# Storing split weights right behind their last part, and adding the last product of gate and up into a bank already read

## The chip, the cores and the metric

The kernel runs on one core of one Trainium2 chip. The metric is device time in microseconds (us) of one execution; lower is better. A core has five engines that run their own instruction lists in order and wait for each other through semaphores: TensorE (PE), VectorE (DVE), ScalarE (ACT), GpSimd (POOL) and SyncE (SP). SP here issues nearly all DMA transfers, on one queue.

## The reference

One block of a transformer in float32: RMSNorm, a projection, differential attention and stick-breaking attention, an output projection, and a SwiGLU feed-forward part. The change touches the feed-forward part alone:

```python
u2 = rms_norm(h, norm2_w)                    # h: 2048 x 1024
gate = einsum('bsd,df->bsf', u2, w_gate)     # 1024 -> 2816
up = einsum('bsd,df->bsf', u2, w_up)         # 1024 -> 2816
h = h + einsum('bsf,fd->bsd', silu(gate) * up, w_down)
```

## The kernel before, in words

Float32 products are made of float16 ones: each operand is scaled by a power of two and split into a high and a low float16 part, and three of the four partial products are summed in PSUM. On top of that the feed-forward part uses a Strassen-like scheme of seven block products in place of eight. It is done in two halves of 1024 tokens. A half goes through eleven groups of 256 feed-forward columns (`fg`), and each group has three weights, called g, u and d after gate, up and down.

In the first half each weight is fetched from the inputs as float32 (`stage`, 1024 KB) into one of the two buffers of the tile `stages`, which the weights take in turn. ACT squares it (tile `sq`, L869 or L184), PE sums the squares of each column (tile `fsc`, L877, or L177 for d), DVE turns the sum into a power of two in some seven small operations (the last one that the split needs is L199), and then the seven block operands are made: high parts on ACT or POOL (L210 on ACT), low parts on DVE (L215), and sums and differences of blocks on POOL (L98, output `stages` or `sx`). The result (`wg`, `wu` or `wd`) is used at once, and is also stored to the DRAM tile `split` (1792 KB), from which the second half loads it without any splitting. A buffer of `stages` may be fetched into again when the last part that reads it is made.

Stores are held in a list, `keep`. A store leaves the list when two later weights have been begun, and it is then put on SP's queue directly behind the fetch just issued (`tc.issue_after`).

`quad` makes the seven products of gate or up for one group: `pa`, `pm`, `pm`, a second product into `pa`, then `pd`, `pm` and `pe`, of 12 matmuls each (L939; a product is 12 matmuls of 128x512). Each of them but the second into `pa` takes a fresh PSUM bank from `pst`, which hands out eight banks in turn. DVE adds the pieces: L952 and L956 for the `pm` pair, L966 reads `pd` into the block c22, L968 adds `pd` to u2, L971 takes the fourth product, L975 adds `pe` to u2. Each of the four finished blocks then goes to SiLU on ACT (gate, L986) or to a multiplication on DVE (up, L1006), and after up four more sums on DVE (L98, outputs `cu` and `cg`) make the operands of down (`act`, L1000 on ACT and L98 on POOL or DVE). Down runs for two or three groups at once (L1041), and its sums go through ACT (L1067), DVE (L1047) and POOL.

The order of the instructions on each engine isn't written by hand. A scheduler sets it from a model of times, and each engine then executes its list strictly in that order: an instruction that waits holds everything behind it.

Of the kernel before, what the change touches and what calls it, by code (L numbers as in the profile page):

```python
# [16 lines left out]
ALU = mybir.AluOpType  # L17
# [4 lines left out]
S, D, P = 2048, 1024, 128  # L22
NT, KT, NC = S // P, D // P, S // 512
FF = 2816
NFG = FF // 256
# [34 lines left out]
def block(tc, a, out):  # L60
    nc = tc.nc
    PE, ACT, DVE, POOL, SP = nc.tensor, nc.scalar, nc.vector, nc.gpsimd, nc.sync
    top = ExitStack()
    with top:
# [100 lines left out]
        split = dr.tile([NFG, 3, P, 7 * 2 * 512], F16, name="split")  # L165
# [637 lines left out]
        with ExitStack() as ph2:  # L803
# [18 lines left out]
            r_2, p_2, r_24 = rp2  # L822
            scales = {}

            keep, rows = [], []
            stages = fw.tile([P, 2, 2048], F32, name="stages", bufs=1)
            turn = [0]

            def stage(fg, nme):
                st = stages[:, turn[0]]  # L830
                turn[0] ^= 1
                f0 = 256 * fg
                with tc.issue_after(rows[1].ins) if (fg, nme) == (1, "u") else nullcontext():
                    d = fetch(st, f0, nme)
                if len(keep) > 1:
                    with tc.issue_after(d.ins):
                        SP.dma_start(*keep.pop(0))
                return st

            def fetch(st, f0, nme):  # L840
                if nme == "d":
                    return SP.dma_start(st.rearrange("p (f n) -> p f n", f=2), a["w_down"][0, f0 : f0 + 256, :].rearrange("(f p) n -> p f n", p=P))
                return SP.dma_start(st.rearrange("p (k n) -> p k n", k=KT), a["w_gate" if nme == "g" else "w_up"][0, :, f0 : f0 + 256].rearrange("(k p) n -> p k n", p=P))

            ones = fw.tile([P, P], BF16, name="ones", bufs=1)
            DVE.memset(ones[:], 1.0)
# [5 lines left out]
            def load_ffn(half, fg, names, W):  # L852
                eng = "ADP" if fg == 0 else WE
                sc = scales.setdefault(fg, {})
                for nme in names:
                    if half == 1:
                        yield
                        late = nme == "d" and fg == NFG - 1
                        w16 = (fd if nme == "d" and not late else fw).tile([P, 7, 2, 512], F16, tag="wd" if nme == "d" and not late else "wgu", bufs=2, name=nm("w" + nme))
# [3 lines left out]
                    st = stage(fg, nme)  # L863
                    r, p, sW = c1(), c1(), c1()
# [35 lines left out]
                    else:  # L900
                        sv = st.rearrange("p (d k f n) -> p d k f n", d=2, k=4, f=2)
                        xv = sx[:].rearrange("p (k n) -> p k n", k=4)
                        wv = w16[:].rearrange("p o s (k n) -> p o s k n", k=4)
# [11 lines left out]
                        putk(4, sv[:, :, :, 0, :], 2)  # L915
                        putk(6, xv.unsqueeze(1), 1)
                    W[nme] = w16
                    keep.append((split[fg, "gud".index(nme)], w16[:].rearrange("p o s n -> p (o s n)")))
                    if fg == NFG - 1 and nme == "d":
                        while keep:  # L920
                            SP.dma_start(*keep.pop(0))
                if half == 0 and "g" in names:
                    kg, F = c1(), c1()
                    times(kg, sc["g"][1], p_2, 2.0 ** -14)
# [10 lines left out]
            def product(ps_, wv, wo, X, xo, start, stop):  # L935
                q = 0
                for kt in range(4):
                    for xi, wi in ((0, 0), (1, 0), (0, 1)):
                        PE.matmul(ps_[:].rearrange("p (t n) -> p t n", n=P), lhsT=wv[:, wo, wi, 128 * kt : 128 * kt + 128], rhs=X[xo][:, :, xi, kt, :], start=start and q == 0, stop=stop and q == 11, skip_group_check=not start)  # L939
                        q += 1  # L940

            def quad(wv, X, tag, bufs, c11, hook=None):
                def cst():
                    return fp.tile([P, 512], F32, tag=tag, bufs=bufs, name=nm(tag))

                pa = pst("pa")
                product(pa, wv, 0, X, 0, True, True)
                u2 = cst()
                ACT.copy(u2[:], pa[:])
                p6 = pst("pm")  # L950
                product(p6, wv, 4, X, 4, True, True)
# [12 lines left out]
                product(pd, wv, 2, X, 2, True, True)  # L964
                c22 = cst()
                DVE.tensor_tensor(c22[:], pd[:], u3[:], ALU.add)  # L966
                c11(1, 1, c22)
                DVE.tensor_tensor(u2[:], u2[:], pd[:], ALU.add)  # L968
                p4 = pst("pm")
                product(p4, wv, 3, X, 6, True, True)  # L970
                DVE.tensor_tensor(u3[:], u3[:], p4[:], ALU.subtract)  # L971
                c11(1, 0, u3)
                p5 = pst("pe")
                product(p5, wv, 5, X, 3, True, True)
                DVE.tensor_tensor(u2[:], u2[:], p5[:], ALU.add)  # L975
                c11(0, 1, u2)

            def gate(W, X, hook=None):
# [256 lines left out]
```

## Time and profile before

| | us |
|---|---|
| median of 3 runs | 2778.39 (2778.34 to 2778.42) |
| the profiled execution | 2775.94 |
| its span, first to last instruction | 2774.2 |
| PE busy in the span | 2494.4 (90%) |
| DVE busy | 2008.2 (72%) |
| ACT busy | 1359.0 (49%) |
| POOL busy | 1428.7 (52%) |

Attention and the projections fill the span to about 1466 us, the first half of the feed-forward part goes to about 2190 us, the second to the end. The profile page says where time is lost on average; a table by stages (windows) says in which part, and the rows in order of time say which instruction waited for which. Times of rows are from the start of the span.

### The profile page before, as it was taken

The page shows a single profiled execution, that of the slowest core. Times are in us where ns is not written, and L with a number is a line of the kernel's source. Part 1 is how long each engine was busy: PE and PEld are TensorE (multiplying, and loading weights), DVE is VectorE, ACT ScalarE, POOL GpSimd, SP SyncE. Part 2 cuts the span into 40 slices and gives each one's busy share as a digit, 9 for nine tenths or more (in the row PEclk, how much of TensorE's full clock was granted, in tenths as well). Part 3 has the DMA queues.
Part 4 walks back from the last instruction along what each step waited for, and adds up shares of the span by engine and source line. Part 5 has one row for each costly group of instructions (what it writes and reads, how often), then busy time and mean ns, then how long its engine had stood idle before and what let it go on. Part 6 is the DMA issues. An engine that isn't in the chain of part 4 may idle for free.

```text
span 2774.2 us, 45434 instructions
## 1 busy us (share of the span) xinstructions
PE 2494.4 (90%) x17084; PEld 1409.7 (51%) x17084; DVE 2008.2 (72%) x3796; ACT 1359.0 (49%) x2539; POOL 1428.7 (52%) x1002
## 2 busy tenths in 40 slices
PE   6998989988888786888889898999899999999999
PEld 4655555555555454557775343444444444444444
DVE  6888879787989989875766877777776644444444
ACT  4665656466878878764644534343442211121120
POOL 2568767665544555546664656564645422322322
PEclk9999999999999997999999999999999999999999
DMA  7788787789999998997797565555648835535432
GB/s 228 198 165 183 145 190 162 173 172 203 198 209 195 199 181 160 191 195 208 198 309 258 199 222 200 197 203 197 231 172 284 349 141 193 205 126 205 183 121 92
DMA packets 646829, 543.52 MB, mean 196 GB/s; under 512 B 506368, under 2 KB 573952, under 8 KB 636368
## 3 DMA queue, kind: packets, MB, share of 16 engines
q1 hardware_dynamic: 644784, 538.53, 71.0%
q8 instruction: 134, 2.20, 0.3%
q0 software_dynamic: 512, 1.36, 0.2%
q10 hardware_dynamic: 1312, 0.72, 0.1%
q14 instruction: 87, 0.71, 0.1%
HBM read 261.08 MB, written 147.32 MB: 147 GB/s over the span
## 4 chain that ended last, share of the span: by engine, by line
PE 31%; DVE 9%; DMA 6%; issue 4%; ACT 3%; POOL 3%; SPq 0%; DVEq 0%; ACTq 0%; POOLq 0%
PE pd L1041 13%; PE pm L939 7%; PE pa L939 5%; PE pd L939 3%; DVE wd L215 2%; PE pe L939 2%; DMA stages<-in_w_gate_dram 2%; DMA stages<-in_w_down_dram 1%; DVE wu L215 1%; PE po L761 1%; DMA aT<-s 1%; DMA stages<-in_w_up_dram 1%; DVE cg L1006 1%; POOL s L98 1%; DVE wg L215 1%
## 5 line engine op out<-in xcount | busy, mean ns | idle before, releaser
L98 POOL TENSOR_TENSOR s<-z,s 128x1024 f16<-128x1024 f32 (+7 forms) x288 | 473.8, 1653 | 336.0 <-ACT s L89 300.0
L320 PE MATMUL pj<-w,xt 128*128 128x384 f16 x3072 | 573.9, 335 | 26.9 <-DVE st L330 11.6
L320 PEld LDWEIGHTS <-xt 128*128 128x128 f16 x3072 | 300.5, 100 | 237.6 <-issue 38.7
L1041 PE MATMUL pd<-wd,act 128*128 128x512 f16 x1764 | 395.4, 382 | 20.2 <-ACT cu L1067 16.9
L448 PE MATMUL sc<-kT,qT 128*128 128x512 f16 (+3 forms) x1280 | 347.9, 362 | 69.8 <-DVE z L558 30.9
L557 DVE TENSOR_TENSOR_SCAN z<-z,sc 128x512 f32<-128x512 f32 (+3 forms) x320 | 355.8, 1113 | 66.2 <-ACT sc L555 62.8
L458 PE MATMUL yp<-v,aT 128*128 128x64 f16 (+1 forms) x4896 | 282.5, 208 | 83.1 <-DMA aT<-s 82.2
L458 PEld LDWEIGHTS <-aT 128*128 128x128 f16 x4896 | 245.7, 102 | 174.3 <-DMA aT<-s 111.6
L939 PEld LDWEIGHTS <-wu 128*128 128x128 f16 x1848 | 182.2, 99 | 243.4 <-issue 12.8
L98 POOL TENSOR_TENSOR act<-cg,act 128x512 f16<-128x512 f32 x109 | 152.7, 1411 | 284.4 <-ACT act L1000 284.4
L939 PEld LDWEIGHTS <-wg 128*128 128x128 f16 x1848 | 181.1, 98 | 221.0 <-issue 6.4
L1041 PEld LDWEIGHTS <-act 128*128 128x128 f16 x1764 | 173.5, 98 | 232.0 <-issue 27.7
L89 ACT CAST s<-z 128x384 f16<-128x384 f32 (+7 forms) x216 | 170.4, 789 | 151.7 <-DMA aT<-s 64.2
L98 POOL TENSOR_TENSOR stages<-stages 128x512 f32<-128x512 f32 x97 | 171.6, 1770 | 129.0 <-DVE wd L215 47.0
L98 POOL TENSOR_TENSOR hs<-hs,cu 128x512 f32<-128x512 f32 x102 | 133.0, 1312 | 188.2 <-DVE cu L1047 64.6
L554 ACT ACTIVATE z<-sc,c 128x512 f32<-128x512 f32 (+3 forms) x320 | 203.1, 635 | 12.6 <-PE sc L448 10.8
L939 PE MATMUL pm<-X,wu 128*128 128x512 f16 x792 | 186.8, 390 | 18.2 <-ACT wu L210 10.8
L1000 ACT CAST act<-cg 128x512 f16<-128x512 f32 x126 | 77.7, 618 | 250.8 <-DVE cg L1006 202.7
L558 DVE TENSOR_TENSOR z<-sc,z 128x512 f32<-128x512 f32 (+3 forms) x320 | 193.6, 607 | 8.1
L555 ACT ACTIVATE sc<-sc,c 128x512 f32<-128x512 f32 (+3 forms) x320 | 195.3, 610 | 0.0
L1047 DVE SCALAR_TENSOR_TENSOR hs<-pd,c,hs 128x512 f32<-128x512 f32 x144 | 105.8, 748 | 118.4 <-PE pd L1041 110.3
L761 PE MATMUL po<-wo,mt 128*128 128x256 f16 x1536 | 180.9, 275 | 9.2 <-DVE xf L764 4.8
(245 smaller groups left out, 4140.7 us busy)
## 6 DMA issues: line engine op xcount, KB each, us to landing
xt<-xs SPq DMA_DIRECT2D x112, 512.0 KB, 4.3
hs<-hd SPq DMA_DIRECT2D x72, 512.0 KB, 4.4
hd<-hs SPq DMA_DIRECT2D x56, 512.0 KB, 5.2
split<-wg SPq DMA_DIRECT2D x11, 1792.0 KB, 10.6
split<-wu SPq DMA_DIRECT2D x11, 1792.0 KB, 10.4
split<-wd SPq DMA_DIRECT2D x11, 1792.0 KB, 10.9
wg<-split SPq DMA_DIRECT2D x11, 1792.0 KB, 7.2
wd<-split SPq DMA_DIRECT2D x11, 1792.0 KB, 9.2
```

Source lines behind the costliest of these rows:

```text
L89: ACT.copy(dst, src)
L98: (DVE if e == "D" else POOL).tensor_tensor(dst, a_, b_, op)
L320: PE.matmul(pj[:, :384], lhsT=xv[:, xi, kt, :], rhs=G["w"][:, wi, kt, :], start=n == 0, stop=n == 23)
L448: PE.matmul(sc[:, : 128 * w].rearrange("p (t n) -> p t n", n=P), lhsT=G["q"][i // 4][:, 2 - 2 * o + m, i % 4, :], rhs=G["k"][q][:, m, 0:w, ...
L458: PE.matmul(yp[:, y0 : y0 + wd], lhsT=aT[:, a_, :], rhs=v[:, v_ : v_ + wd], start=start and j == 0 and q == 0, stop=stop and j == nb - 1 a ...
L554: ACT.activation(om[:, lo:hi], sc[:, :w], AF.Sigmoid, scale=G["nkz"][:])
L555: ACT.activation(sc[:, :w], sc[:, :w], AF.Sigmoid, scale=G["kz"][:])
L557: DVE.tensor_tensor_scan(ov, ov, sc[:, :w], om[:, hi : hi + 1], op0=ALU.mult, op1=ALU.bypass)
L558: DVE.tensor_tensor(be[:, lo:hi], sc[:, :w], om[:, lo + 1 : hi + 1], ALU.mult)
L761: PE.matmul(po[:, sl], lhsT=mt[:, kt, P * xi : P * xi + P], rhs=wos[2 * h + n][wi][:, kt, :], start=q == 0, stop=q == 23)
L939: PE.matmul(ps_[:].rearrange("p (t n) -> p t n", n=P), lhsT=wv[:, wo, wi, 128 * kt : 128 * kt + 128], rhs=X[xo][:, :, xi, kt, :], start=st ...
L1041: PE.matmul(po[:], lhsT=act[:, ao, xi, 128 * j : 128 * j + 128], rhs=W["d"][:, wo, wi, :], start=start and u == 0 and q == 0, stop=u == nu ...
```

## The change

Two edits. A store of a split weight is issued where the split ends in the program, without the list and without a place on the queue behind a fetch. And the last product of `quad` is added by PE into `pd`, which DVE has read for c22 by then; the separate addition of `pd` to u2 (old L968) goes, the addition of `pe` to u2 becomes one of `pd` (new L968), and `quad` takes five banks instead of six.

```diff
-            keep, rows = [], []
+            rows = []
...
                 with tc.issue_after(rows[1].ins) if (fg, nme) == (1, "u") else nullcontext():
-                    d = fetch(st, f0, nme)
-                if len(keep) > 1:
-                    with tc.issue_after(d.ins):
-                        SP.dma_start(*keep.pop(0))
+                    fetch(st, f0, nme)
                 return st
...
                     W[nme] = w16
-                    keep.append((split[fg, "gud".index(nme)], w16[:].rearrange("p o s n -> p (o s n)")))
-                    if fg == NFG - 1 and nme == "d":
-                        while keep:
-                            SP.dma_start(*keep.pop(0))
+                    SP.dma_start(split[fg, "gud".index(nme)], w16[:].rearrange("p o s n -> p (o s n)"))
...
                 c11(1, 1, c22)
-                DVE.tensor_tensor(u2[:], u2[:], pd[:], ALU.add)
                 p4 = pst("pm")
                 product(p4, wv, 3, X, 6, True, True)
                 DVE.tensor_tensor(u3[:], u3[:], p4[:], ALU.subtract)
                 c11(1, 0, u3)
-                p5 = pst("pe")
-                product(p5, wv, 5, X, 3, True, True)
-                DVE.tensor_tensor(u2[:], u2[:], p5[:], ALU.add)
+                product(pd, wv, 5, X, 3, False, True)
+                DVE.tensor_tensor(u2[:], u2[:], pd[:], ALU.add)
                 c11(0, 1, u2)
```

The scheduler makes a new order of it on every engine of the feed-forward part. Lines of the changed kernel have other numbers: L837 (store) is L916, L841 and L839 are the fetches, L961 is the old L966, L965 the old L971, L999 the old L1006, L867 the old L869.

SP's queue in the first half, from the fetch of a gate weight on, before:

```order
L843 DMA stages<-in_w_gate_dram 128x8x256
L837 DMA split<-wd_23047 128x7168
L842 DMA stages<-in_w_down_dram 128x2x1024
L837 DMA split<-wu_23145 128x7168
L843 DMA stages<-in_w_up_dram 128x8x256
L837 DMA split<-wg_23287 128x7168
```

and now:

```order
L916 DMA split<-wd_23022 128x7168
L841 DMA stages<-in_w_gate_dram 128x8x256
L916 DMA split<-wu_23118 128x7168
L839 DMA stages<-in_w_down_dram 128x2x1024
L916 DMA split<-wg_23258 128x7168
L841 DMA stages<-in_w_up_dram 128x8x256
```

Fetch and store have changed places in each pair: the same store stood behind the fetch and now stands ahead of it.

DVE at the end of up, where the parts of `wd` are made between the sums of up, before:

```order
L966 TENSOR_TENSOR cu_22150<-pd_22137,cu_22086 128x512
L968 TENSOR_TENSOR cu_22057<-cu_22057,pd_22137 128x512
L215 SCALAR_TENSOR_TENSOR wd_22103<-stages,c_21913,wd_22103 128x2x512
L1006 SCALAR_TENSOR_TENSOR cg_21711<-cu_22150,c_21430,cg_21711 128x512
L215 SCALAR_TENSOR_TENSOR wd_22103<-stages,c_21913,wd_22103 128x2x512
L215 SCALAR_TENSOR_TENSOR wd_22103<-sx_22113,c_21913,wd_22103 128x512
L971 TENSOR_TENSOR cu_22086<-cu_22086,pm_22156 128x512
L975 TENSOR_TENSOR cu_22057<-cu_22057,pe_22173 128x512
L1006 SCALAR_TENSOR_TENSOR cg_21675<-cu_22086,c_21430,cg_21675 128x512
L878 TENSOR_REDUCE m_22203<-fsc_22202 128x1
L1006 SCALAR_TENSOR_TENSOR cg_21646<-cu_22057,c_21430,cg_21646 128x512
L215 SCALAR_TENSOR_TENSOR wd_22103<-stages,c_21913,wd_22103 128x2x512
```

and now:

```order
L961 TENSOR_TENSOR cu_22133<-pd_22120,cu_22069 128x512
L215 SCALAR_TENSOR_TENSOR wd_22086<-stages,c_21896,wd_22086 128x2x512
L999 SCALAR_TENSOR_TENSOR cg_21696<-cu_22133,c_21418,cg_21696 128x512
L215 SCALAR_TENSOR_TENSOR wd_22086<-stages,c_21896,wd_22086 128x2x512
L215 SCALAR_TENSOR_TENSOR wd_22086<-sx_22096,c_21896,wd_22086 128x512
L965 TENSOR_TENSOR cu_22069<-cu_22069,pm_22138 128x512
L876 TENSOR_REDUCE m_22184<-fsc_22183 128x1
L999 SCALAR_TENSOR_TENSOR cg_21661<-cu_22069,c_21418,cg_21661 128x512
L195 TENSOR_SCALAR m_22184<-m_22184 128x1
L215 SCALAR_TENSOR_TENSOR wd_22086<-stages,c_21896,wd_22086 128x2x512
L170 TENSOR_SCALAR c_22116<-m_22184 128x1
L968 TENSOR_TENSOR cu_22040<-cu_22040,pd_22120 128x512
```

The sum into u2 and the multiplication behind it (L968 and an L999) now stand behind the last part of `wd`, not ahead of it.

ACT a little later, while gate of the next group runs and the parts of `wu` are made, before:

```order
L949 COPY cg_22244<-pa_22231 128x512
L1000 CAST act_22043<-cu_22188 128x512
L1000 CAST act_22043<-cg_21646 128x512
L1000 CAST act_22043<-cg_21689 128x512
L869 ACTIVATE sq_22294<-stages 128x2048
L1000 CAST act_22043<-cg_21675 128x512
L210 ACTIVATE wu_22201<-stages,c_22134 128x2x512 x2
L210 ACTIVATE wu_22201<-sx_22218,c_22134 128x512
L986 ACTIVATE cg_22287<-pa_22231,c_21905 128x512
L986 ACTIVATE cg_22309<-cg_22309,c_21905 128x512
L210 ACTIVATE wu_22201<-stages,c_22134 128x2x512
```

and now:

```order
L993 CAST act_22026<-cu_22169 128x512
L210 ACTIVATE wu_22182<-stages,c_22117 128x2x512 x2
L210 ACTIVATE wu_22182<-sx_22199,c_22117 128x512
L993 CAST act_22026<-cg_21632 128x512
L993 CAST act_22026<-cg_21675 128x512
L993 CAST act_22026<-cg_21661 128x512
L979 ACTIVATE cg_22269<-pa_22213,c_21889 128x512
L867 ACTIVATE sq_22275<-stages 128x2048
L210 ACTIVATE wu_22182<-stages,c_22117 128x2x512
```

The squares of the gate weight (`sq`), which wait for its fetch, now stand behind the first parts of `wu`. The parts of `wd` that follow pass the squares of the next up weight in the same way: all of them in every second stretch, all but the last one in the others. On PE the last product of `quad` stands later in the list: 3 to 11 matmuls of the following product or of down come ahead of it.

More of the change, by code (lines that the diff above doesn't have):

```diff
@@ L841, in fetch @@
                 if nme == "d":
-                    return SP.dma_start(st.rearrange("p (f n) -> p f n", f=2), a["w_down"][0, f0 : f0 + 256, :].rearrange("(f p) n -> p f n", p=P))
-                return SP.dma_start(st.rearrange("p (k n) -> p k n", k=KT), a["w_gate" if nme == "g" else "w_up"][0, :, f0 : f0 + 256].rearrange("(k p) n -> p k n", p=P))
+                    SP.dma_start(st.rearrange("p (f n) -> p f n", f=2), a["w_down"][0, f0 : f0 + 256, :].rearrange("(f p) n -> p f n", p=P))
+                else:
+                    SP.dma_start(st.rearrange("p (k n) -> p k n", k=KT), a["w_gate" if nme == "g" else "w_up"][0, :, f0 : f0 + 256].rearrange("(k p) n -> p k n", p=P))
             ones = fw.tile([P, P], BF16, name="ones", bufs=1)
```

## The prediction

> **What bounds the kernel now.** I first read the table by stages, because the change touches the feed-forward part alone (columns: stretch, length, busy us and count of PE, PEld, DVE, ACT, POOL; granted clock, DMA share, GB/s).
>
> ```profile
> span 2774.2 us, 45434 instructions
> ...
> 1700.00:1800.00 100.00, 91.27 (x427) 42.04 (x427) 76.12 (x111) 40.50 (x49) 57.81 (x38) 0.98 0.59 206
> 1800.00:1900.00 100.00, 93.36 (x435) 43.13 (x433) 71.34 (x102) 39.14 (x46) 59.29 (x39) 0.97 0.63 223
> 1900.00:2000.00 100.00, 88.62 (x411) 40.31 (x409) 80.15 (x112) 44.93 (x55) 61.36 (x40) 0.97 0.55 187
> ...
> 2300.00:2400.00 100.00, 100.00 (x465) 45.37 (x464) 45.08 (x59) 18.97 (x30) 29.16 (x23) 1.00 0.49 177
> ```
>
> The second half is PE without a gap. The first half leaves PE idle for 7 to 11 us in 100, with no other engine full, so something there is late. The rows of PE in order of time name it (start, us, instruction, and in brackets the idle time ahead and what ended it). They are one stretch: up of one group, gate and up of the next, gate again, then down.
>
> ```profile
> 1794.07 0.60 PE L939 MATMUL pm<-X,wu 128*128 128x512 f16 x2 [2.88 <-ACT wu L210]
> ...
> 1796.46 6.36 PE L939 MATMUL pm<-X,wu 128*128 128x512 f16 x22 [1.78 <-DVE wu L215]
> ...
> 1816.06 1.03 PE L877 MATMUL fsc<-sq,ones 128*128 128x256 bf16 x8 [1.15 <-ACT sq L869]
> ...
> 1839.82 1.24 PE L1041 MATMUL pd<-wd,act 128*128 128x512 f16 x5 [0.93 <-ACT cg L986]
> ...
> 1845.61 13.18 PE L1041 MATMUL pd<-wd,act 128*128 128x512 f16 x49 [4.55 <-ACT cu L1067]
> ```
>
> That is 11.3 us of waiting in a stretch, all for weights being split or for ACT behind them. There are five such stretches. The chain of waits shows what the weights wait for (start, us, what):
>
> ```profile
> 1758.15 2.59 PE pa L939 x12
> ...
> 1777.28 6.60 DMA stages<-in_w_gate_dram
> ...
> 1796.43 6.44 DMA stages<-in_w_down_dram
> ...
> 1807.36 6.66 DMA stages<-in_w_up_dram
> ...
> 1830.48 6.71 DMA stages<-in_w_gate_dram
> ```
>
> Four fetches of a stretch lie on the chain. Each starts the moment its buffer's last part is made, so the weights go round: fetch, squares, scale, parts, fetch. A product of 12 matmuls takes PE 2.59, or 0.216 a matmul.
>
> **The second half: nothing.** The edit to the sums applies there too. The rows of one product and its readers:
>
> ```profile
> 2310.56 2.75 PE L939 MATMUL pm<-X,wu 128*128 128x512 f16 x12
> ...
> 2310.82 0.69 DVE L966 TENSOR_TENSOR cu<-pd,cu 128x512 f32<-128x512 f32 x1 [1.89 <-PE pd L939]
> ```
>
> DVE has read `pd` by 2311.5, and the product ahead of the last one runs to 2313.15. That covers the new wait by 1.6 us, and the new order puts more matmuls in between. The 22 additions that go there save DVE 22 x 0.68, while DVE is 45% busy: no gain. Were the cover gone, each quad would pay at most the 0.69.
>
> **The price of a store ahead of a fetch.** SP's rows, and the page's row for that store (median time to landing last):
>
> ```profile
> 1777.28 0.38 SPq L843 DMA_DIRECT2D stages<-in_w_gate_dram  x1
> 1777.71 0.57 SPq L837 DMA_DIRECT2D split<-wd  x1
> ...
> split<-wd SPq DMA_DIRECT2D x11, 1792.0 KB, 10.9
> ```
>
> The fetch lands at 1777.28 + 6.60 = 1783.9, the store behind it at about 1777.71 + 10.9 = 1788.6. So the store holds the queue for some 4.7 us, less a little that overlaps: I take 4.6. With the places changed, a fetch lands 6.6 + 4.6 = 11.2 us after its buffer is free. The low bound is nothing (both share the queue and the fetch's packets get through at once), the high one 0.57 for the issue and 4.7. Nothing waits for the stores themselves.
>
> **What the new order gives back.** The rows that I move, of DVE and ACT:
>
> ```profile
> 1764.26 0.68 DVE L968 TENSOR_TENSOR cu<-cu,pd 128x512 f32<-128x512 f32 x1
> ...
> 1771.20 0.67 DVE L975 TENSOR_TENSOR cu<-cu,pe 128x512 f32<-128x512 f32 x1
> ...
> 1773.73 1.42 DVE L1006 SCALAR_TENSOR_TENSOR cg<-cu,c,cg 128x512 f32<-128x512 f32 x1
> ...
> 1775.08 2.17 DVE L215 SCALAR_TENSOR_TENSOR wd<-stages,c,wd 128x1024 f16<-128x1024 f32 x1
> ...
> 1783.22 0.14 DVE L199 TENSOR_SCALAR c<-c 128x1 f32<-128x1 f32 x1
> ...
> 1783.96 1.91 ACT L869 ACTIVATE sq<-stages 128x2048 bf16<-128x2048 f32 x1 [2.95 <-DMA stages<-in_w_gate_dram]
> ...
> 1786.29 2.19 ACT L210 ACTIVATE wu<-stages,c 128x1024 f16<-128x1024 f32 x2
> ...
> 1791.54 0.68 DVE L966 TENSOR_TENSOR cg<-pd,cg 128x512 f32<-128x512 f32 x1
> ...
> 1794.05 2.35 DVE L215 SCALAR_TENSOR_TENSOR wu<-stages,c,wu 128x1024 f16<-128x1024 f32 x1 [0.64 <-ACT wu L210]
> ...
> 1802.95 1.91 ACT L184 ACTIVATE sq<-stages 128x2048 bf16<-128x2048 f32 x1 [1.32 <-DMA stages<-in_w_down_dram]
> ...
> 1806.05 1.28 DVE L215 SCALAR_TENSOR_TENSOR wg<-stages,c,wg 128x1024 f16<-128x1024 f32 x1 [0.96 <-ACT wg L210]
> ...
> 1814.10 1.91 ACT L869 ACTIVATE sq<-stages 128x2048 bf16<-128x2048 f32 x1 [5.45 <-DMA stages<-in_w_up_dram]
> ...
> 1816.42 2.19 ACT L210 ACTIVATE wd<-stages,c 128x1024 f16<-128x1024 f32 x2
> ...
> 1825.04 1.64 DVE L98 TENSOR_TENSOR cg<-cg,cg 128x512 f32<-128x512 f32 x1
> ...
> 1828.28 2.18 DVE L215 SCALAR_TENSOR_TENSOR wd<-stages,c,wd 128x1024 f16<-128x1024 f32 x1
> ...
> 1838.16 0.68 DVE L966 TENSOR_TENSOR cg<-pd,cg 128x512 f32<-128x512 f32 x1
> ```
>
> I walk through this stretch in the new order with these durations, on the old clock.
>
> 1. The last part of `wd` loses L968, L975 and an L1006 ahead of it: 0.6 + 0.6 + 1.3. It ends at 1774.8 instead of 1777.25. The gate fetch lands at 1774.8 + 11.2 = 1786.0 instead of 1783.9.
> 2. The scale of `wu` (L199) no longer has the sums after up ahead of it, some 4.7 us, and comes near 1778.5 instead of 1783.2. ACT makes the first parts of `wu` at once, where before it stood 2.95 at the squares. The last part ends near 1792.1 instead of 1796.4.
> 3. PE gains that wait but meets two others in front of the last product: for the squares, which end at 1788, and for L966, which DVE reaches behind the parts of `wu`, near 1789.8. PE goes on with up's `pm` at 1793.9 and is done with it at 1799.1, against 1802.7.
> 4. The down fetch lands at 1792.1 + 11.2 = 1803.3, against 1802.9. Its squares end at 1805.4, and PE, which is earlier now, waits for them 2.4 to 3.9 us. The last part of `wg` stands behind them on ACT, so it ends at 1807.8, against 1807.3.
> 5. The up fetch lands at 1819.0, against 1814.0; its column sum cannot start before 1821. In every second stretch (B) PE's list holds 39 matmuls of gate ahead of that sum and waits hardly at all, in the others (A) 18, and PE waits 5.4.
> 6. The parts of `wd` no longer stand behind these squares on ACT, or only the last does. The last one ends at 1819.9 (B) or 1824.3 (A) against 1830.5. The sums after up follow on DVE (three L98 like the row at 1825.04, one of 1.4, an L1006 of 1.5, L952 and L956 of 0.6: 9 us with POOL beside them), then the scale and the first parts of `wu`, then L966: at 1836.5 (B) or 1840.9 (A) against 1838.2.
> 7. Gate's last product must wait for that L966, which it did not. It ends at 1839.1 or 1843.5; 12 matmuls later PE is where the old row at 1845.61 starts: 1841.7 or 1846.1.
>
> So B is 3.9 us ahead and A 0.5 us behind; 1.7 a stretch on the mean. Down then runs on PE alone and covers the rest, the two fetches in it included. Five stretches give 8.5 us. The profiled execution would be 2775.94 - 8.5 = 2767.4; the median of the runs stands 2.45 above it, so 2778.39 - 8.5 = **2770**. An error of 3 us in a stretch is easily made here, which is 15 in the sum: 2755 to 2785 for this case alone.
>
> What I cost at nothing: the 22 additions less in the first half beyond those in step 1, as DVE waits for ACT or PE around them; and a bank less a quad, since the one wait for a bank in the rows (4.55, for ACT's L1067) is set by ACT.
>
> PE's clock weighs against the change. After the 4.55 us wait 49 matmuls took 13.18 us and not 10.6, and after 2.88 and 1.78 the 22 took 6.36 and not 4.75. The Trainium skill (TensorE: Matmul & The Clock Gate, Part 1: The HAM clock gate) says that an idle window of about 3.4 us halves the clock, and a busy one of that length restores it. By it a wait costs up to 1.7 more as an estimate, and new waits of 3.9 and 5.4 would cost it again; the two rows above agree with such a price. In my sum the price stands on both sides alike.
>
> **Rivals.**
>
> *The parts do not get ahead* (slower). If DVE or POOL brings the first parts of `wu` no earlier than 1786, step 2 gives nothing. The last part ends at 1796.4, down lands at 1807.6, `wg` ends at 1812.1, up lands at 1823.3, and the column sum starts at 1825 instead of 1816. PE has 11 (A) or 32 (B) matmuls more to do ahead of it than the 7 of before, 2.4 or 6.9 us, so it loses 6.6 or 2.1, and L966 comes later behind it: about 5 a stretch, 25 in all, 2803. For it: DVE is 71 to 80% busy. Against it: ACT stood idle 2.95 and 5.45 at those squares.
>
> *Cold PE* (slower). The waits are as I say, but in more places: two waits over 3 us in each stretch cost 1.5 to 2.5 each, by the two rows above. About +4 in place of -1.7: 20 more, 2790.
>
> *No change.* The end of a stretch is set by gate's last sums, SiLU and ACT's L1067, and these come when they did: 2778.
>
> *More than I say* (faster). The packets share the queue and fetches land only 2 us later, so that half of the 11.3 us a stretch goes: 5 x 5.6 = 28, 2750. The trace speaks against it: the store behind a fetch needed 4.7 more.
>
> *The change does not do what it says.* A store on SP that waits for parts would hold up the fetch behind it. It waits for the same last part as the fetch, so nothing is added but the queue's time, counted above.
>
> **How the numbers follow.** Forecast 0.40, parts not ahead 0.13, cold PE 0.15, no change 0.18, more 0.14. I call 0.2%, 5.6 us, what can be told from no change. The forecast's own range gives 0.29 faster, 0.06 within and 0.05 slower; the others add 0.14 faster, 0.17 within, 0.29 slower (the two slower ones, and 0.01 of no change). That is 0.43, 0.23 and 0.34. The range leaves out the ends of the first and last rivals: 2753 to 2797.
>
> **What would show it.** Right: in the profile after, fetches land about 11 us after issue and their stores in about 6; the wait of PE for `wu` is gone; a wait for `sq` or `pd`'s reader stands in front of L939 and L877; the second half still shows PE at 100.00. Wrong: fetches still land in 6.6; `wu` still makes PE wait; the waits of a stretch sum to more than 14.

## The result and the profile after

The changed kernel takes 2749.81 us (median of 4 runs, 2747.07 to 2752.86) where the kernel before, run beside it, takes 2778.36: a ratio of 0.9899, with a 95% interval of 0.9882 to 0.9916. Run again later it took 2746.51, a ratio of 0.9900 (0.9879 to 0.9920). The forecast was 2770 with a range from 2753: the sign is right, the gain of 28.5 us is more than three times the 8.5 forecast.

The two profiled executions can't be subtracted as they stand, since the output projection ahead of the changed part ended at different times. Its last 120 matmuls, first in the kernel before, then in the changed kernel, then in the changed kernel's later run (start, us, instruction, wait ahead):

```profile
1453.60 13.26 PE L761 MATMUL po<-wo,mt 128*128 128x256 f16 x120 [1.13 <-DVE wo L764]
```

```profile
1457.94 13.26 PE L761 MATMUL po<-wo,mt 128*128 128x256 f16 x120 [1.14 <-DVE wo L764]
```

```profile
1448.63 13.26 PE L761 MATMUL po<-wo,mt 128*128 128x256 f16 x120 [1.14 <-DVE wo L764]
```

The spans end at 2774.2, 2751.1 and 2738.6. Behind this point they last 1320.6, 1293.2 and 1290.0: the changed part is 27.4 to 30.6 us shorter. Of the 12.5 us between the two profiles of the changed kernel, 9.3 lie ahead of this point. So I compare from here on by stretches: from one fetch of a gate weight to the same one two groups later. The table of windows (stretch, length, busy us and count of PE, PEld, DVE, ACT, POOL; granted clock, DMA share, GB/s), before:

```profile
1650.19:1777.28 127.09, 115.82 (x542) 53.25 (x541) 95.77 (x138) 52.58 (x62) 73.74 (x48) 0.97 0.57 203
1777.28:1906.00 128.72, 117.43 (x542) 53.76 (x541) 95.33 (x138) 52.59 (x62) 73.20 (x48) 0.96 0.57 200
1906.00:2032.40 126.40, 115.02 (x538) 52.86 (x537) 94.94 (x138) 52.59 (x62) 72.15 (x47) 0.97 0.60 204
```

and after:

```profile
1652.70:1774.52 121.82, 116.39 (x542) 54.09 (x540) 92.67 (x133) 52.42 (x62) 73.87 (x49) 0.97 0.61 212
1774.52:1894.51 119.99, 115.15 (x542) 53.39 (x540) 92.82 (x133) 52.27 (x62) 72.40 (x49) 0.99 0.62 215
1894.51:2014.99 120.48, 113.45 (x542) 52.89 (x540) 93.96 (x133) 51.99 (x62) 73.15 (x49) 1.00 0.62 214
```

The first and the third are stretches of the kind A, the second is a B. On the mean a stretch fell from 127.4 to 120.8, by 6.6 and not by 1.7. Of that 5.5 is time in which PE waited (length less busy: 11.3 before, 5.8 now), and 1.1 is PE's own work, the same instructions (538 to 542 of them on record) done in less time on a higher granted clock (0.96 to 0.97 before, 0.97 to 1.00 now). Three such stretches are 19.9 us; 1.8 lie between the projection and the first of them (196.6 to 194.8), and 5.7 behind the third (741.8 to 736.1).

All waits of PE above 0.1 us in one stretch of each kind after, where the kernel before had those quoted in the prediction. First B, then A:

```profile
1787.03 1.67 PE L934 MATMUL pm<-X,wu 128*128 128x512 f16 x7 [1.66 <-ACT cg L979]
...
1803.42 0.49 PE L177 MATMUL fsc<-id,m 128*128 128x128 f32 x2 [2.12 <-ACT sq L184]
1803.75 4.31 PE L934 MATMUL pd<-X,wu 128*128 128x512 f16 x12
...
1829.62 3.83 PE L1034 MATMUL pd<-wd,act 128*128 128x512 f16 x17
1834.39 2.75 PE L934 MATMUL pd<-X,wg 128*128 128x512 f16 x12 [0.94 <-DVE cg L961]
1836.97 13.33 PE L1034 MATMUL pd<-wd,act 128*128 128x512 f16 x61
...
1908.82 0.60 PE L875 MATMUL fsc<-sq,ones 128*128 128x256 bf16 x4 [1.95 <-ACT sq L867]
...
1923.42 0.49 PE L177 MATMUL fsc<-id,m 128*128 128x128 f32 x2 [0.40 <-ACT sq L184]
...
1936.11 1.46 PE L1034 MATMUL pd<-wd,act 128*128 128x512 f16 x6 [3.56 <-DVE cu L968]
1938.68 1.03 PE L875 MATMUL fsc<-sq,ones 128*128 128x256 bf16 x8 [1.12 <-ACT sq L867]
```

No wait for `wu` is left. The row at 1834.39 is gate's last product: it now stands between 17 and 61 matmuls of down, in the place where PE waited 4.55 for ACT's L1067 before, and that wait is gone too. What came in their place are waits for squares (`sq`) and for DVE's sums, and in B one of 1.66 for a SiLU (L979). The fetches and stores (median time from issue to landing, last column):

```profile
split<-wg SPq DMA_DIRECT2D x11, 1792.0 KB, 6.9
split<-wu SPq DMA_DIRECT2D x11, 1792.0 KB, 6.7
split<-wd SPq DMA_DIRECT2D x11, 1792.0 KB, 6.8
...
stages<-in_w_gate_dram SPq DMA_DIRECT2D x11, 1024.0 KB, 9.5
stages<-in_w_up_dram SPq DMA_DIRECT2D x11, 1024.0 KB, 10.2
stages<-in_w_down_dram SPq DMA_DIRECT2D x11, 1024.0 KB, 8.9
```

A fetch lands 8.9 to 10.2 after its issue and not 11.2; a store in 6.7 to 6.9. The second half is PE without a gap as before:

```profile
2300.00:2400.00 100.00, 100.00 (x465) 45.35 (x464) 39.85 (x54) 16.82 (x26) 30.07 (x24) 1.00 0.48 177
```

### The profile page after: what moved, and what is told of

Its sections match the earlier page's. It is cut to its first block, busy times and chain, and to the rows that moved or that the text cites. A ratio compares the mean times of both kernels' runs of the same rounds, so it can differ in the third digit from the quotient of the medians.

```text
span 2751.1 us, 45381 instructions
## 1 busy us (share of the span) xinstructions
PE 2489.3 (90%) x17084; PEld 1411.3 (51%) x17084; DVE 1967.9 (72%) x3752; ACT 1357.8 (49%) x2539; POOL 1428.8 (52%) x1002
## 4 chain that ended last, share of the span: by engine, by line
PE 33%; DVE 7%; DMA 6%; POOL 3%; issue 3%; ACT 2%; SPq 0%; DVEq 0%; POOLq 0%; ACTq 0%
PE pd L1034 12%; PE pm L934 7%; PE pd L934 6%; PE pa L934 5%; DVE wd L215 2%; DMA stages<-in_w_down_dram 1%; DMA aT<-s 1%; POOL stages L98 1%; PE po L761 1%; POOL s L98 1%; DMA X<-xcd 1%; DMA stages<-in_w_up_dram 1%; DVE wu L215 1%; DVE cg L98 1%; DVE cg L999 1%
## 5 line engine op out<-in xcount | busy, mean ns | idle before, releaser
L934 PEld LDWEIGHTS <-wg 128*128 128x128 f16 x1848 | 181.3, 98 | 224.4 <-issue 10.9
L1034 PEld LDWEIGHTS <-act 128*128 128x128 f16 x1764 | 172.8, 98 | 217.0 <-issue 10.9
L554 ACT ACTIVATE z<-sc,c 128x512 f32<-128x512 f32 (+3 forms) x320 | 203.5, 636 | 10.7 <-PE sc L448 5.9
L934 PE MATMUL pm<-X,wu 128*128 128x512 f16 x792 | 179.3, 379 | 1.8 <-ACT cg L979 1.7
```

Of the source, the lines that this page charges most:

```text
L554: ACT.activation(om[:, lo:hi], sc[:, :w], AF.Sigmoid, scale=G["nkz"][:])
L1034: PE.matmul(po[:], lhsT=act[:, ao, xi, 128 * j : 128 * j + 128], rhs=W["d"][:, wo, wi, :], start=start and u == 0 and q == 0, stop=u == nu ...
```

## The experiments

Each verdict is a ratio to the kernel before, run on the same chip. "Stretch" is the mean of three stretches between the same gate fetches in that kernel's profile, 127.4 before and 120.8 (120.5 in the later run) after.

### Each edit alone

The stores alone: the changed kernel with the old sums.

```diff
+                DVE.tensor_tensor(u2[:], u2[:], pd[:], ALU.add)
                 p4 = pst("pm")
...
-                product(pd, wv, 5, X, 3, False, True)
-                DVE.tensor_tensor(u2[:], u2[:], pd[:], ALU.add)
+                p5 = pst("pe")
+                product(p5, wv, 5, X, 3, True, True)
+                DVE.tensor_tensor(u2[:], u2[:], p5[:], ALU.add)
```

> The changed kernel with the old sums: the store stands ahead of the fetch, but the last product of gate and up takes a bank of its own again and u2 takes pd in an addition of its own. Theory 1 (the order of the queue, and the places of the weights' parts ahead of the squares on ACT that go with it, bring the time): 2749.8 stays nearly, 2750 to 2758, and PE's wait for wu is gone. Theory 2 (the sums bring it: DVE has two operations less between the parts, the last part of wd ends earlier, a bank less makes down wait less): 2770 to 2780, with the wait for wu back. Theory 3 (each edit takes one wait away, and the clock stays up only when both are gone): 2760 to 2770.

2755.79 us, 0.9920 (0.9905 to 0.9935), 21 us faster; stretch 122.9.

The sums alone: the kernel before with the second hunk of the change and nothing else.

> The kernel before with the new sums alone: stores stand behind the fetches as they did. Theory 1 (queue and order): 2772 to 2780. Theory 2 (sums): 2750 to 2758. Theory 3 (both needed): 2765 to 2775. If a fetch behind a store costs anything on the path, the best of the three would be here, below 2750, since the sums are new and fetches land in 6.6 us.

2761.78 us, 0.9944 (0.9927 to 0.9962), 15 us faster; stretch 127.1.

The stores alone came out as theory 1 has it; with the sums alone none of the three ranges was met. Each edit brings over half of the gain alone, and the two don't add to 36. How the waits change hands shows in one stretch B of each. PE's rows with the stores alone:

```profile
1793.60 0.49 PE L177 MATMUL fsc<-id,m 128*128 128x128 f32 x2 [1.45 <-ACT sq L184]
...
1818.85 6.42 PE L1036 MATMUL pd<-wd,act 128*128 128x512 f16 x29
1830.47 12.68 PE L1036 MATMUL pd<-wd,act 128*128 128x512 f16 x49 [5.20 <-ACT cu L1062]
```

and with the sums alone:

```profile
1782.92 5.28 PE L939 MATMUL pd<-X,wg 128*128 128x512 f16 x12 [4.16 <-DVE cg L966]
...
1822.04 2.54 PE L1039 MATMUL pd<-wd,act 128*128 128x512 f16 x11
1830.61 4.04 PE L939 MATMUL pd<-X,wg 128*128 128x512 f16 x12 [6.03 <-DVE cg L966]
```

With the stores alone the waits for `wu` go, and ACT's L1062 (the old L1067) in front of down stays, 5.20. With the sums alone that one goes, and the new wait of gate's last product for DVE's reading of `pd` takes its place, 4.16 and 6.03, with a slower clock behind it (12 matmuls in 5.28 and 4.04 instead of 2.75; the granted clock from 1782.92 to 1786.50 was 0.50). A stretch then is no shorter than before; what this kernel gains lies ahead of the stretches (190.6 from the projection to the first gate fetch, against 196.6) and behind them (735.7 against 741.8). With both edits the product has its place in down's gap and, in this B, waits 0.94.

### What in the sums: additions, bank, or place

Three kernels undo parts of the second edit in the changed kernel. The first takes a sixth bank that nobody uses:

```diff
+                pst("pe")
                 product(pd, wv, 5, X, 3, False, True)
```

> The changed kernel, but each quad of gate and up takes a sixth bank again, which nobody uses; the last product still adds into pd and the addition on DVE stays saved. Theory 1 (the five banks bring the sums' share of the gain: down's first products no longer meet a bank that ACT's L1062 has to read): the share is lost, 2755 to 2758, the time of the stores alone, and PE waits some 4.5 us for ACT at down again. Theory 2 (the saved DVE additions, and the place of those that remain, bring it): 2747 to 2753, as the changed kernel.

2745.42 us, 0.9892 (0.9876 to 0.9909); stretch 121.7. The second gives DVE its addition back:

```diff
                 c11(1, 1, c22)
+                DVE.tensor_tensor(u2[:], u2[:], pd[:], ALU.add)
...
-                product(pd, wv, 5, X, 3, False, True)
+                product(pd, wv, 5, X, 3, True, True)
```

> The changed kernel, but the last product starts anew in pd's bank, and pd is added to u2 before it as in the kernel before: five banks, and DVE's two additions a quad as before (44 additions of 0.68 us in all, 22 of them in the first half). Theory 1 (banks): 2747 to 2753. Theory 2 (additions): 2755 to 2758. If the wait for DVE's reading of pd is on the path in every stretch, the additional reading ahead of the last product costs 0.7 for each gate and up of the first half, up to 22 x 0.7 = 15 us: 2765 at most.

2747.76 us, 0.9900 (0.9882 to 0.9919); stretch 121.1. The third undoes both:

> The changed kernel with the sums' savings both undone: two additions a quad on DVE and six banks as before; what stays of the edit is that the last product is written into pd's bank and so must come behind DVE's two readings of it. Theory 1 (the gain of the sums lies in the place that this wait gives the last product, behind the first products of down): 2745 to 2752. Theory 2 (bank and additions each suffice by themselves, and one of them is needed): 2755.8, as the stores alone.

2744.01 us, 0.9885 (0.9868 to 0.9901); stretch 121.4. And the same in the kernel before, with the stores behind the fetches:

> The kernel before, with the last product written into pd's bank behind DVE's two readings, and nothing else: six banks, two additions, stores behind the fetches. Theory 1 (the sums' share comes from the place that the last product must take): the time of the sums alone, 2757 to 2765 (0.992 to 0.996). Theory 2 (without the stores edit the additions or the bank count after all): 2770 to 2780.

2765.19 us, 0.9961 (0.9947 to 0.9975); stretch 126.5. The first three are as fast as the changed kernel, and the fourth keeps most of what the sums bring alone: its interval reaches from 0.9947 to 0.9975, that of the sums from 0.9927 to 0.9962. So neither the 22 additions saved in the first half nor the bank bring anything that can be told. What is left is the one thing these kernels share: the last product is written where DVE reads, so it must come behind these readings, and every engine gets another order. The kernel of `wait_only` takes six banks a quad and does all the old additions on DVE, and nothing is lost; its interval lies clear of that of the stores alone (0.9905 to 0.9935).

### What the late fetch costs

Half of the store's size, so that a fetch comes sooner:

```diff
-                    SP.dma_start(split[...], w16[:].rearrange("p o s n -> p (o s n)"))
+                    SP.dma_start(split[...][:, :3584], w16[:].rearrange("p o s n -> p (o s n)")[:, :3584])
```

> The changed kernel with half of each split weight stored (896 KB in place of 1792), and this half loaded twice in the second half of the tokens: the other half of the weights is wrong there, but all transfers of the second half have their size. A fetch behind the store should land some 2.2 us sooner (half of 4.3 to 4.6). Theory a (what is left of PE's waits, 4.7 to 7.0 a stretch, comes from late fetches): two of these waits shrink by 2 each, 5 x 4 = 20 us less, about 2730. Theory b (the fetches are covered by PE's work, and the waits are set by ACT and DVE): 2745 to 2755.

2746.60 us, 0.9890 (0.9875 to 0.9904); stretch 122.6. The fetches land far sooner than I had put it, since SP issues most of the half stores well ahead of them (the first at 1761.90, the fetch at 1767.37):

```profile
stages<-in_w_gate_dram SPq DMA_DIRECT2D x11, 1024.0 KB, 5.3
stages<-in_w_up_dram SPq DMA_DIRECT2D x11, 1024.0 KB, 5.3
stages<-in_w_down_dram SPq DMA_DIRECT2D x11, 1024.0 KB, 4.8
```

This is a fetch by itself: 4.8 to 5.3. The time is the one that theory b gave, but this run can't decide between the theories, because its order isn't that of the changed kernel. On ACT and DVE its instructions stand, over the three stretches, as in the kernel with the sums alone, but for a record or two: down's squares are ahead of the first parts of `wg`. The sums alone and the half store, one under the other:

```profile
1788.82 1.91 ACT L184 ACTIVATE sq<-stages 128x2048 bf16<-128x2048 f32 x1 [4.40 <-DMA stages<-in_w_down_dram]
...
1790.73 2.17 ACT L210 ACTIVATE wg<-stages,c 128x1024 f16<-128x1024 f32 x2
```

```profile
1788.89 1.91 ACT L184 ACTIVATE sq<-stages 128x2048 bf16<-128x2048 f32 x1 [2.82 <-DMA stages<-in_w_down_dram]
...
1790.80 2.17 ACT L210 ACTIVATE wg<-stages,c 128x1024 f16<-128x1024 f32 x2
```

In this order the landing does count. With fetches of 6.5 to 6.6 us (the sums alone) a stretch takes 127.1 and the kernel 2761.78; with fetches of 4.8 to 5.3 it takes 122.6 and 2746.60. The bytes stored differ too, so the whole of the 15 us isn't shown to be the fetch's.

Then three kernels that put one of the three stores back behind its fetch and leave the other two ahead, here for gate's (the store leaves the list right behind the next fetch of up):

```diff
-                    SP.dma_start(split[fg, "gud".index(nme)], w16[:].rearrange("p o s n -> p (o s n)"))
+                    if nme == "g" and fg < NFG - 2:
+                        keep.append(...)
+                    else:
+                        SP.dma_start(split[...], ...)
```

> The changed kernel, but the store of gate's weights stands behind the fetch of up again; the orders of ACT and DVE stay nearly those of the changed kernel. The up fetch should land some 3 us sooner (10.2 to near 7). Theory a (the late up fetch is on the path where up's column sum is waited for, in every second stretch: 3.56 and 1.12 us there): these waits shrink by 3 in 2 or 3 stretches, 6 to 9 us less, 2740 to 2744. Theory b (the fetches are covered, as the half store suggests): 2747 to 2753.

2743.61 us, 0.9882 (0.9864 to 0.9900); stretch 120.0. Since a few us can't be told across separate runs, it was run beside the changed kernel:

> The changed kernel with gate's store behind the fetch of up, as before, now beside the changed kernel. Theory a (the late up fetch is on the path in every second stretch, where its waits of 4.7 became 2.0 and 1.7): 3 to 6 us faster than the changed kernel. Theory b (covered): within 3 us of it.

> The changed kernel once more, beside the next one on the same chip: 2744 to 2752, a ratio to before of 0.988 to 0.992.

2746.22 against 2746.51, ratios 0.9894 (0.9874 to 0.9913) and 0.9900 (0.9879 to 0.9920): no difference that can be told, each interval being some 5 us wide on either side. The up fetch lands in 6.6 instead of 10.1, with 5 of ACT's 62 instructions in an A in other places and 1 in a B. The waits change hands: in one A the wait of 3.57 for L968 goes, and 1.77 for the reader of `pd` and 1.3 more for squares come. For down's store:

> The same for the store of down's weights and the fetch of gate (9.5 to near 6.6); here the order of ACT moves too. Theory a: the waits for gate's squares (1.95 in every second stretch, 1.66 for a SiLU that stands with them in the other) go, 2 us in each of 5 stretches: 2738 to 2743. Theory b: 2747 to 2753.

2751.07 us, 0.9914 (0.9894 to 0.9933); stretch 121.0; no gain again, in another order of ACT and DVE. For up's store, with the down fetch landing in 6.4 instead of 8.9:

> The same for the store of up's weights and the fetch of down (8.9 to near 6.6). Theory a: the wait for down's squares (2.12 us in one kind of stretch, with 1.5 lost on the cold clock behind it, and 0.40 in the other) goes: 2 or 3 times 3.6, 7 to 11 us less, 2739 to 2743. Theory b: 2747 to 2753.

2761.81 us, 0.9954 (0.9938 to 0.9969), 12 to 15 us slower than the changed kernel; stretch 125.1. The fetch lands sooner and the kernel is slower, which neither theory had. ACT's rows show what else is different. The changed kernel, from up's `wu` to the end of `wg` (start, us, instruction):

```profile
1794.60 2.19 ACT L210 ACTIVATE wg<-stages,c 128x1024 f16<-128x1024 f32 x2 [0.59 <-issue]
...
1801.37 1.91 ACT L184 ACTIVATE sq<-stages 128x2048 bf16<-128x2048 f32 x1 [3.50 <-DMA stages<-in_w_down_dram]
...
1803.28 1.13 ACT L210 ACTIVATE wg<-stages,c 128x1024 f16<-128x1024 f32 x1
```

With up's store behind the fetch:

```profile
1797.19 1.91 ACT L184 ACTIVATE sq<-stages 128x2048 bf16<-128x2048 f32 x1 [5.35 <-PE pm L940]
...
1799.71 2.17 ACT L210 ACTIVATE wg<-stages,c 128x1024 f16<-128x1024 f32 x2
...
1806.20 1.15 ACT L210 ACTIVATE wg<-stages,c 128x1024 f16<-128x1024 f32 x1 [3.23 <-POOL stages L98]
```

The first parts of `wg` stand behind down's squares there, and ahead of them in the changed kernel. The last part of `wg`, which frees the buffer for the up fetch, comes later for it: from the down fetch to the up fetch are 18.6 us (1790.52 to 1809.13), against 13.8 (1792.49 to 1806.31). This isn't the old order come back: in the kernel before, the first parts of `wg` stood ahead of the squares too, which began at 1802.95, and 10.9 us lay between the two fetches:

```profile
1798.36 2.19 ACT L210 ACTIVATE wg<-stages,c 128x1024 f16<-128x1024 f32 x2 [0.60 <-DVE c L199]
```

With up's store behind the fetch, the squares have the place that they have with the sums alone and in the half store, where it was cheap when the down fetch landed in 4.8. So, as these rows read, neither the landing nor the order has a price by itself; what counts is whether the squares that ACT does first have their fetch by then. That this one place makes up the 12 to 15 us is likely and not shown, since other instructions moved as well (7 of ACT's 62 in an A, 3 in a B). That the scheduler, seeing a later fetch in its model, puts the parts first is how I read it; the model's times weren't looked at.

More lateness than this does cost. The same store is issued twice, and the fetch stands behind both:

```diff
+                    second.append(SP.dma_start(split[...], ...))
```

> The changed kernel with each split weight stored twice, both stores ahead of the fetch: a fetch should land 4.3 us later than in the changed kernel, some 14 us after its issue. Theory a (fetches are on the path, through the squares): two or three waits for squares in a stretch grow by 4.3 each, 5 x 9 to 5 x 13 = 43 to 65 us more than the 2767.7 or 2749.8 of the kernels with one store ahead: 2793 to 2833. Theory b (PE has other work, as the half store, where fetches landed in 5 us and the time stayed, suggests): not over 2775.

2802.59 us, 1.0096 (1.0081 to 1.0111), 53 us more than the changed kernel; stretch 132.5. The second store didn't queue up as I thought: SP holds it until the first has landed (its waits in the first half name DMA into `split`, 43.4 us in 7 times for `wd`), I take it because both write the same place. The fetch is issued some 6 us late and lands 9.3 to 10.0 after that. Theory a's size is right, and one of PE's waits stands where it says:

```profile
1815.74 0.80 PE L177 MATMUL fsc<-id,m 128*128 128x128 f32 x2 [6.12 <-ACT sq L184]
```

But 10 to 18 of ACT's 62 instructions of a stretch have other places here, so how much of the 53 us is lateness and how much is order wasn't separated.

A second store behind the fetch, where ACT and DVE have the changed kernel's orders in all three stretches:

> The changed kernel, each split weight stored twice; the second store stands behind the fetch on the queue, and the orders of ACT and DVE are nearly those of the changed kernel. Theory a (the queue works its transfers off one after the other, so that only what stands ahead of a fetch makes it late): fetches land as in the changed kernel, 9 to 10 us, and the time is 2748 to 2756. Theory b (transfers of the queue share the engines, and a store behind a fetch makes it later too): fetches land in 12 to 14 us, 3 us later each, and some of the three fetches of a stretch are on the path: 2765 to 2800.

2767.74 us, 0.9971 (0.9960 to 0.9981). The fetches land as in the changed kernel (9.5, 10.4, 8.9) and a stretch takes 122.0, so of theory a the landing came true and the time didn't. It is a mild test of the queue: SP issues the second store when the first has landed, 6.4 us after the fetch (1774.12 and 1780.51), and so it meets only the fetch's last third. Most of what was lost lies at the two ends, 10 us between the projection and the first gate fetch (205.0 against 194.8) and 10 behind the third stretch (745.7 against 736.1). At the first end PE stands at

```profile
1486.02 4.56 PE L935 MATMUL pd<-X,wg 128*128 128x512 f16 x12 [7.53 <-DMA X<-xcd]
```

The load of `X` is issued behind a store of `wd` there, 29.4 us after the start of the projection's last matmuls (1476.97 less 1447.59); in the changed kernel it is 14.2 (1472.17 less 1457.94). Neither theory had that.

The stores on ACT's queue:

```diff
-                    SP.dma_start(split[...], ...)
+                    ACT.dma_start(split[...], ...)
```

> The changed kernel with the stores issued by ACT, on a queue of its own. A fetch then doesn't stand behind a store: it should land in 6 to 7 us, if the two queues share the 16 engines evenly, against 9 to 10. Theory a (late fetches cost what is left of the waits): 2735 to 2745. Theory b (fetches are covered): 2748 to 2756. Theory c (ACT stands at each store until the last part is made, and holds the copies and squares behind it): 2765 to 2790.

2810.77 us, 1.0128 (1.0111 to 1.0145); stretch 134.7. Median times to landing:

```profile
split<-wu ACTq DMA_DIRECT2D x11, 1792.0 KB, 8.2
...
stages<-in_w_gate_dram SPq DMA_DIRECT2D x11, 1024.0 KB, 9.9
stages<-in_w_up_dram SPq DMA_DIRECT2D x11, 1024.0 KB, 10.7
stages<-in_w_down_dram SPq DMA_DIRECT2D x11, 1024.0 KB, 9.1
```

Issued in the same moment on two queues (at 1786.32 and 1786.33, for one), fetch and store share the engines, and the fetch lands no sooner than behind the store. The Trainium skill (DMA: Bandwidth & Descriptors, Issuing engines are not separate DMA queues) says that queues of several issuing engines run on the same DMA engines; these rows agree. The order is once more that of the sums alone: DVE's instructions stand as there but for a record or two, and ACT's but for the stores, one copy and a record or two. Down's squares, ahead of the first parts of `wg`, wait longest here:

```profile
1813.41 1.91 ACT L184 ACTIVATE sq<-stages 128x2048 bf16<-128x2048 f32 x1 [8.39 <-DMA stages<-in_w_down_dram]
...
1815.32 2.17 ACT L210 ACTIVATE wg<-stages,c 128x1024 f16<-128x1024 f32 x2
```

So three kernels have nearly one order on ACT and DVE and three landings: 4.8 to 5.3 us (with half the bytes stored), 6.5 to 6.6 and 9.1 to 10.7, with stretches of 122.6, 127.1 and 134.7. The changed kernel's fetches land in 8.9 to 10.2, and its stretch takes 120.8: its order covers a lateness that this one pays for. What the stores cost ACT itself (theory c) wasn't taken apart from it.

### Both pieces that seemed best

> Gate's store behind the fetch of up, and the last product written into pd's bank with two additions and six banks as in the run that left the wait only. If the two add: 2738 to 2742. If what is left of PE's waits is set by the order of DVE and ACT: 2743 to 2749, no different from either.

2759.11 us, 0.9950 (0.9930 to 0.9969); stretch 126.2. Two edits that each left the time as it was cost 13 us together. The expectation was wrong on both sides: the order again is another one. No kernel of these beats the changed one by more than can be told.

## Why the prediction was right or wrong

**The direction and the mechanism were right; one step and one price were not, and they hold most of what the forecast missed.** Parts of a weight pass the squares on ACT, the buffer comes free earlier, the wait for `wu` goes, and gate's last product fills the gap ahead of L1067; that is what the rows show, in the places named. The steps on the old clock (the changed kernel's times less 0.24 in B and 120.23 in A, so that the products after up's first one start together):

| step | predicted | measured |
|---|---|---|
| 1: last part of `wd` | 1774.8 | 1773.9 |
| 2: scale of `wu`, its last part | 1778.5, 1792.1 | 1777.0, 1791.8 |
| 3: PE done with up's `pm` pair | 1799.1 | 1798.3 |
| 4: down lands, last part of `wg` | 1803.3, 1807.8 | 1801.1, 1805.6 |
| 5: up lands (A) | 1819.0 | 1816.5 |
| 6: last part of `wd` | B 1819.9, A 1824.3 | 1819.5, 1822.4 |
| 6: gate's L966 done | B 1836.5, A 1840.9 | 1834.1, 1832.7 |
| 7: where the old row at 1845.61 starts | B 1841.7, A 1846.1 | 1839.3, 1839.8 |

**The step that failed is 6, in A, by 8 us.** I took 16.6 us from the last part of `wd` to L966 in both kinds of stretch: 9 of sums after up, then scale and parts. In B it was 14.6. In A it was 10.3:

```profile
1937.05 1.65 DVE L98 TENSOR_TENSOR cu<-cg,cg 128x512 f32<-128x512 f32 x1
1938.73 1.65 DVE L98 TENSOR_TENSOR cg<-cg,cg 128x512 f32<-128x512 f32 x1
1940.30 2.29 DVE L215 SCALAR_TENSOR_TENSOR wd<-stages,c,wd 128x1024 f16<-128x1024 f32 x1
...
1952.23 0.68 DVE L961 TENSOR_TENSOR cg<-pd,cg 128x512 f32<-128x512 f32 x1
```

In A the part waits for late squares, and half of the sums that I put behind it are done ahead of it. I had carried B's order over to A and moved it as a block: a delay on ACT was passed on in full to DVE's later work, which in truth fills the time. PE reached gate's last product with no wait (1954.87), 6.3 us ahead of my time for it, and A came out like B. Of the 8 us, 1.9 come from the last part of `wd`, made at 1822.4 and not at 1824.3, and 6.3 from the sums. Over the stretches A, B, A my terms give 2.9 us in all, where 19.9 were measured.

**"The price stands on both sides alike" failed too, by some 2.5 us in B and 1.1 on the mean.** In B the kernel before lost 1.6 behind the wait at 1796.46 and 2.6 behind that of 4.55, where my estimate had at most 1.7 for a wait. After, only the 12 matmuls at 1803.75 are slow (4.31, next start 4.10 later instead of 2.59: 1.5 lost), and the 61 behind gate's last product run at 0.218 each. So B is 6.3 earlier at the old row by the table, and some 2.5 more behind it: 8.8, where the stretch shows 128.72 - 119.99 = 8.7. Over three stretches PE's busy time says 1.1 a stretch.

**The price of a fetch behind a store was too high, 11.2 for 8.9 to 10.2**; in A it is behind the 1.9 us above, as the up fetch landed 2.5 us sooner than in step 5. I added the store's 4.6 to the 6.6 that a fetch took; but those 6.6 already hold a delay by the store behind it, as a fetch by itself takes 4.8 to 5.3.

**Right:** nothing in the second half; the saved additions at nothing (`fresh_pd`) and the bank at nothing (`extra_bank`, `wait_only`); waits for squares and for `pd`'s reader as the new waits; nearly, step 4's wait of 2.4 to 3.9, measured 2.12 in B (0.40 in A). Step 3's two waits ahead of gate's last product didn't come so: in B PE stood 1.66 for a SiLU there and then had none, in A 1.95 for the squares. Step 5's 5.4 in A became 3.56 for L968 and 1.12 for the squares.

**The rivals.** *More than I say* came nearest: it gave 2750 with half of the waits gone, and 11.3 became 5.8. Its reason, fetches only 2 us later, doesn't carry the number: they landed 2.4 to 3.5 later, and the waits went because parts passed squares and gate's last product took L1067's gap, so its hit is in part luck. *No change* and *cold PE* failed: L1067's wait is gone, and the granted clock rose. *The parts do not get ahead* looks like up's store alone, where parts of `wg` fall behind the squares. The table of what would show it right (stores in about 6, no wait for `wu`, waits for `sq` and `pd`'s reader, second half full) was met, with fetches nearer to 10 than to 11.

What stays open is what the changed kernel's order would bring with earlier fetches, why two edits that each leave the time alone cost 13 us together, and how much of the 15 us of the sums alone is the same place of the last product at the two ends of the first half, which no run took apart.

## What to carry to other kernels

Where a scheduler sets the order, price a changed transfer by its landing and by the order that comes out of it on the engines that consume it, together: here fetches that landed 2.5 to 5 us sooner left the time as it was or went with 12 to 15 us more, and in one fixed order 1.3 to 1.7 us sooner went with 15 us less. Compare the orders of two runs before reading their difference as the transfer's price. When walking a new order by hand, walk each kind of stretch with its own rows, and let work that is free to run fill a delay instead of passing the delay on. Undo parts of an edit one by one before naming what it saves: the additions and the bank that the second edit saves brought nothing that can be told, which leaves the place that it forces on one product.

## What the runs showed of the hardware that was not expected

A transfer is slowed by what stands behind it in its queue. The same 1024 KB fetch took 4.8 to 5.3 us by itself, 6.5 to 6.7 with a 1792 KB store behind it, and 8.9 to 10.2 with the store ahead; the store took 10.2 to 10.9 behind the fetch and 6.7 to 6.9 ahead of it. Changing their places moved the fetch by 2.4 to 3.5, not by the store's 4.6. A store that came 6.4 us behind the fetch didn't slow it (`second_store`).

A wait of the same length cost PE's clock different amounts. The six matmuls behind a wait of 3.56 or 3.57 us for L968 (L969 in `second_store`) took 1.46 in the changed kernel (granted clock 1.00 from 1936.10 to 1938.60), 2.72 in `second_store`, and 1.86 in the changed kernel's later run (0.69 from 1923.50 to 1926.00):

```profile
1923.53 1.86 PE L1034 MATMUL pd<-wd,act 128*128 128x512 f16 x6 [3.57 <-DVE cu L968]
```

while a wait of only 2.12 cost 1.5. The Trainium skill (TensorE: Matmul & The Clock Gate, Part 1: The HAM clock gate) says that the window in which the clock's gate watches for idle time runs freely; the rows agree, in that the length of a wait alone doesn't set its price.
